# Two more expert lists unsplit: a branch on the lists' lengths and a ring of nine raw buffers

## The chip, the cores and the metric

One NeuronCore of a Trainium2 chip runs the whole program. The metric is device time in microseconds (us) of one execution. TensorE does the matmuls, VectorE (DVE) and ScalarE (ACT) the elementwise work, SyncE's queue (SP) issues the transfers.

## The reference, cut to what matters

A two-layer transformer block over 256 latent tokens and 256 context tokens with 1024 features, all in float32. The second layer ends with a mixture of eight experts on the 256 latent tokens, and the final norm follows it:

```python
logits = h @ router                              # 256 x 8
top_val, top_idx = top_k(logits, 2)
gate = one_hot(top_idx) weighted by softmax(top_val)
out = sum over e of gate[:, e] * ((silu(h @ w1[e]) * (h @ w3[e])) @ w2[e])
```

w1 and w3 are 1024 x 3584 and w2 is 3584 x 1024 for each expert, so all experts together have 352 MB of weights. Each token goes to two experts. With the given inputs the reference's router sends 53 tokens to expert 0; the lists of the other seven have 143, 68, 63, 55, 48, 44 and 38 tokens in order of length.

## The kernel before, in words

The dense part (both mixers, the first layer's FFN, the router) takes the first half of the time; the change leaves it alone. The expert stage follows.

**Slots.** Slot 0 is always expert 0, so that its weights can be fetched before the lists are known. Slots 1 to 7 are the other experts by falling length of list; `rank()` (L921) works out this order on DVE and leaves it in `oi`, and in `ci` by how much each list is too long for its slot. `CAPS` (L35) gives the places of each slot: slots 0, 2 and 3 have one block of 128 rows, slot 1 has blocks of 128 and 64, slots 4 to 7 have 64. Lists that are longer than their slots would be done in a second pass behind a test at the end (L1285), which here is skipped.

**Chunks.** A slot's 3584 hidden features are done in seven chunks of 512. A chunk needs six transfers of 1 MB each (w1 and w3 in two halves each, w2 in two halves), each into one raw buffer of 128 x 2048 floats; there are seven raw buffers.

**Split chunks** (slots 0 to 3). A raw buffer is split into a high part (ACT, L147) and a remainder (DVE, L152), both 2048 wide (`self.wide`), in six w buffers, so in three pairs. For a block of 128 rows `up` (L1087) and `down` (L1125) do three products (high by high, high by low, low by high) and four steps each, so 12 matmuls of 128x512 for a raw buffer; the block of 64 rows carries high and low rows side by side and takes 8. The first matmul of a buffer needs the low part.

**Paired (unsplit) chunks** (slots 4 to 7). `up_pair` (L1057) and `down_pair` (L1078) multiply the raw floats directly, two weight tiles at once in the two halves of the array's columns. The profile shows two records for each such matmul, so 16 records for a call. No conversion is needed; the raw buffer is free when its matmuls are done.

**Order of the work.** `ORDER` (L38) is written out by hand: (slot, number of chunks). Slot 1, which has most matmuls, is strewn between the paired chunks, while slots 0, 2 and 3 run in one piece. Within a step `slots` (L1140) does the hidden activations of the chunk before (`hidden`), the first product, a part of the previous chunk's `down`, and so on; the framework orders each engine's instructions from this. A slot's tokens are gathered by one-hot matmuls (L995) three steps ahead and its outputs are put back into `X` by `combine` or `combine_pair` at its last chunk. `ytile` gives the four PSUM tiles for outputs: a split slot of one block holds two of them over its seven chunks, a paired slot one, and slot 1 takes two for a moment in each `down`.

**The start.** Expert 0 needs no ranking: `places` builds its one-hot matrix, the gather follows, and `rank()`, the second half of `rows` and `gates` are done on DVE beside slot 0's matmuls.

Of the kernel before, what the change touches and what calls it, by code (L numbers as in the profile page):

```python
# [66 lines left out]
NTS = P + 24  # L67
# [8 lines left out]
class Net:  # L76
    def __init__(self, ctx, tc, I, out):
        self.ctx, self.tc, self.nc, self.I, self.out = ctx, tc, tc.nc, I, out
        nc = self.nc
        self.uid = 0  # L80
        self.const = ctx.enter_context(tc.tile_pool(name="const", bufs=1))
        self.cst = self.const.tile([P, NCST], F32, name="cst")
        self.tab = self.const.tile([P, NTA], F32, name="tab")
        self.X = self.const.tile([P, KT, NT], F32, name="X")
        self.mod = [self.const.tile([P, 48, 2], F32, name=f"mod{l}") for l in range(2)]
        self.amp = [[self.const.tile([P, KT, 2], F32, name=f"amp{l}{i}") for i in range(2)] for l in range(2)]
        self.sc = self.const.tile([P, KT, 32], F32, name="sc")
# [9 lines left out]
        self.nw = 0  # L97
        self.ndq = 0
# [32 lines left out]
    def raw(self, src, n=2048):  # L131
        pool, kw = self.stile("raw", F32, 3, 0)
        t = pool.tile([P, 2048], F32, name=self.nm("raw"), **kw)
        self.dq().dma_start(t[:, :n], src)
        return t
# [5 lines left out]
    def split(self, t, n=2048, step=1024):  # L141

        if self.wide:
            hi, lo = self.wtile("whi"), self.wtile("wlo")
            for c in range(0, n, self.wide):
                c = slice(c, c + self.wide)
                self.nc.scalar.activation(hi[:, c], t[:, c], AF.Copy)  # L147
                self.nw += 1

                at = self.urgent if self.nw <= 2 else self.urgent2 if self.nw <= 5 else None  # L150
                with self.tc.issue_after(at) if at else nullcontext():
                    self.nc.vector.tensor_sub(lo[:, c], t[:, c], hi[:, c].bitcast(F32))  # L152
# [768 lines left out]
    def rank(self):  # L921
# [3 lines left out]
        io8, low, over = tab[:, P:P + 8], tab[:, P + 8:P + 16], tab[:, P + 16:P + 24]  # L925
# [24 lines left out]
        self.oi, self.ci = mk("oi", [P, NE], I32), mk("ci", [P, NE + 1], I32)  # L950
        nc.vector.tensor_copy(self.oi, order)
        more = mk("more", [P, NE + 1])
        nc.vector.tensor_sub(more[:, :NE], count, over)
        nc.vector.tensor_scalar(more[:, :NE], more[:, :NE], 0.0, None, ALU.max)
        nc.vector.reduce_sum(more[:, NE:], more[:, :NE], AX.X)
        nc.vector.tensor_copy(self.ci, more)
        for n, v, at in (("sp", pm, self.spos), ("sg", gate, self.sgate)):
            for tt in range(2):
                r = by_slot(f"{n}{tt}", v[:, tt])
                at[tt] += [r[:, q:q + 1] for q in range(1, NE)]  # L960

    def places(self, s, base, width):
# [3 lines left out]
        sp = mo.tile([P, 4], F32, tag="spb" if s == 1 else "sp", name=self.nm("spb"), bufs=2)  # L966
# [8 lines left out]
    def gather(self, s, base, width, first=None, whole=False):  # L975
# [5 lines left out]
        G, sp = first or self.places(s, base, width)  # L981
        GT = mo.tile([P, NL], F32R, tag="GT" + big, name=self.nm("GT"), bufs=2)
# [6 lines left out]
        for part in range(KT // nk):  # L989
            pool, tag = (aux, "x") if part == 0 or not first else (self.hpp, "h")  # L990
# [8 lines left out]
            if whole:  # L999
                self.acopy(xs[0][:, sl], v)  # L1000
            elif width == P:
                ins = self.to_parts(xs[0][:, sl], xs[1][:, sl], v)
                if first and part == 1:
                    self.urgent2 = ins.ins
            else:
                self.to_parts(xs[0][:, sl, :64], xs[0][:, sl, 64:], v)
        if first:
            with self.tc.issue_after(self.urgent):
                self.gates()
# [46 lines left out]

    def up_pair(self, expert, j, kh, x, ps):  # L1057

        mm = self.nc.tensor.matmul
        ws = [self.raw(self.I["moe"][expert, j, 2 * wi + kh]) for wi in range(2)]  # L1060
# [17 lines left out]
    def down_pair(self, expert, j, h, y):  # L1078

        mm = self.nc.tensor.matmul  # L1080
        ws = [self.raw(self.I["moe"][expert, j, 4 + n]) for n in range(2)]
# [5 lines left out]
    def up(self, expert, j, wi, kh, blocks, pss):  # L1087
# [4 lines left out]
        ws = self.weights(self.I["moe"][expert, j, 2 * wi + kh])  # L1092
# [7 lines left out]
    def hidden(self, acts):  # L1100
# [3 lines left out]
        for a in acts:  # L1104
            pt = self.hpp.tile([P, 512], F32, tag="h", name=self.nm("ht"))
            hh = mo.tile([P, 4, P], F32R, tag="hh", name=self.nm("hh"), bufs=3)
# [18 lines left out]
    def down(self, expert, j, n, parts, y, first, last):  # L1125

        mm = self.nc.tensor.matmul
        ws = self.weights(self.I["moe"][expert, j, 4 + n])
# [11 lines left out]
    def slots(self, l, steps, order, caps, base=0, first=None):  # L1140
# [4 lines left out]
        def start(s):  # L1145
            if s and len(self.spos[0]) == 1:
                self.rank()
            if s not in order:
                order[s] = nc.values_load(self.oi[0:1, s:s + 1], engines=[mybir.EngineType.SP], min_val=0, max_val=NE - 1)
            if s not in state:  # L1150
                state[s] = dict(blocks=[self.gather(s, base + b * P, w, None if state else first, paired(caps[s]))
                                        for b, w in enumerate(caps[s])])
# [92 lines left out]

        self.wide = 1024
        for n in range(2):
            finish(todo, n)
        self.wide = 2048

    def experts(self, cx, l, ps):
# [3 lines left out]
        self.extra = (mo, 4, 3)  # L1255
        self.wide = 2048
# [3 lines left out]
        mk("GT", 2, [P, NL], F32R)  # L1260
        mk("sp", 2, [P, 4], F32)
# [4 lines left out]
        mk("rawx", 4, [P, 2048], F32)  # L1266
        self.tabr = mo.tile([P, NTR], F32, name="tabr2")
        mk("wx", 3, [P, 2048], F32R)
# [8 lines left out]
        steps = []  # L1277
        nxt = [0] * NE
        for e, n in ORDER:
            steps += [(e, nxt[e] + i) for i in range(n)]  # L1280
            nxt[e] += n
        self.slots(l, steps, order, CAPS, first=first)
        self.finish()
# [68 lines left out]
def _constants():  # L1352
# [22 lines left out]
    ts[:, P + 16:] = OVER  # L1375
# [112 lines left out]
```

## Time and profile before

| what | us |
|---|---|
| median of three runs (lowest, highest) | 2052.01 (2050.22, 2052.18) |
| the profiled execution's own time | 2054.98 |
| its span, first to last instruction | 2053.2 |
| first gather of the expert stage starts | 980.49 |
| first expert matmul starts | 986.49 |

Times inside an execution count from the first instruction. A busy TensorE is not TensorE at its peak, so a busy share says less than the spacing of equal instructions. The granted clock (PEclk) is given as a share of full speed, 1.00 for 2.4 GHz and 0.50 for 1.2 GHz; a share between is a mean over a stretch with both.

### The profile page before, as it was taken

Reading aid. Unit: us, or ns where it says so; the run is one execution under the profiler, and the core shown is the slowest. Engines: PE = TensorE matmul, PEld = TensorE weight load, DVE = VectorE, ACT = ScalarE, POOL = GpSimd, SP = SyncE. Lnnn points to the kernel's source line nnn. Section 1 sums busy time; section 2 is a strip of 40 time slices with the busy share of each in tenths; the row PEclk is TensorE's granted clock in tenths of the full one; section 3 lists DMA queues with packets and bytes.
Section 4 is the critical chain, followed back from the end, with each engine's and each line's share of the span. In section 5 each row is a group of like instructions: output and inputs, shape, how many; then the busy total and the mean of one; then the engine's idle time right before and its main releaser. Section 6 shows DMA issues by size and latency. Waiting matters only on the chain.

```text
span 2053.2 us, 23609 instructions
## 1 busy us (share of the span) xinstructions
PE 1950.6 (95%) x9254; PEld 1330.5 (65%) x9254; DVE 1030.3 (50%) x1650; ACT 818.6 (40%) x1063; POOL 0.2 (0%) x4
## 2 busy tenths in 40 slices
PE   6999999999999999999899998999999998998996
PEld 4865547778888888557786554554786554784553
DVE  6584455533333367755886222232785224874233
ACT  4574244422222246735674212132674123662121
POOL 0000000000000000000000000000000000000000
PEclk9998999999999999999999999999999999999999
DMA  8310354432322143235898768889997888888783
GB/s 312 129 53 21 113 213 177 185 125 83 131 96 71 62 170 103 87 150 211 312 359 343 297 280 350 344 327 403 355 348 305 327 350 357 336 331 343 289 346 127
DMA packets 68807, 478.43 MB, mean 233 GB/s; under 512 B 7760, under 2 KB 8912, under 8 KB 13392
## 3 DMA queue, kind: packets, MB, share of 16 engines
q1 hardware_dynamic: 68112, 473.03, 59.7%
q10 hardware_dynamic: 576, 3.80, 0.5%
q8 instruction: 75, 1.23, 0.2%
q14 instruction: 44, 0.36, 0.0%
HBM read 475.76 MB, written 1.05 MB: 232 GB/s over the span
## 4 chain that ended last, share of the span: by engine, by line
PE 90%; DVE 4%; ACT 2%; DMA 2%; issue 1%; SPq 0%; ACTq 0%; DVEq 0%
PE ph L1097 18%; PE ph L1063 9%; PE y L1134 9%; PE pf L173 6%; PE pf L175 6%; PE pf L174 6%; PE y L1084 5%; PE pp L175 3%; PE pp L173 3%; PE pp L174 3%; PE ada L200 2%; DVE wlo L152 2%; PE ds L653 2%; PE px L995 1%; ACT whi L147 1%; PE po L173 1%
## 5 line engine op out<-in xcount | busy, mean ns | idle before, releaser
L152 DVE TENSOR_TENSOR wlo<-raw,whi 128x2048 fp32r<-128x2048 f32 x168 | 380.9, 2288 | 198.3 <-ACT whi L147 197.6
L147 ACT ACTIVATE whi<-raw 128x2048 fp32r<-128x2048 f32 x168 | 317.5, 1911 | 59.9 <-PE ph L1097 37.2
L1097 PE MATMUL ph<-whi,xg 128*128 128x512 f32 x1008 | 334.7, 405 | 0.0
L1097 PE MATMUL ph<-wlo,xg 128*128 128x512 f32 x560 | 232.3, 415 | 26.7 <-DVE wlo L152 26.7
L160 DVE TENSOR_TENSOR w<-raw,w 128x1024 fp32r<-128x1024 f32 (+2 forms) x142 | 155.8, 1102 | 179.8 <-ACT w L159 179.6
L159 ACT ACTIVATE w<-raw 128x1024 fp32r<-128x1024 f32 (+2 forms) x142 | 135.5, 961 | 228.8 <-PE pf L175 152.6
L1097 PEld LDWEIGHTS ph<-whi,xg 128*128 128x128 f32 x1008 | 196.4, 195 | 45.6
L1063 PE MATMUL ph<-raw,xn 128*64 128x512 f32 x896 | 223.5, 603 | 2.4 <-DMA raw<-in_moe 2.4
L1097 PEld LDWEIGHTS ph<-wlo,xg 128*128 128x128 f32 x560 | 109.0, 195 | 60.8 <-issue 30.7
L1063 PEld LDWEIGHTS ph<-raw,xn 128*64 128x64 f32 x896 | 64.6, 137 | 115.1 <-issue 108.9
L173 PE MATMUL pf<-fhhi,w 128*128 128x512 f32 x352 | 137.2, 391 | 1.5 <-ACT fhhi L304 1.5
L174 PE MATMUL pf<-fhlo,w 128*128 128x512 f32 x352 | 137.0, 389 | 0.0
L175 PE MATMUL pf<-fhhi,w 128*128 128x512 f32 x352 | 137.0, 389 | 0.0
L1134 PE MATMUL y<-wlo,hh 128*128 128x512 f32 x280 | 113.5, 405 | 6.6 <-DVE wlo L152 6.6
L1084 PE MATMUL y<-raw,hn 128*64 128x512 f32 x448 | 109.9, 596 | 0.9 <-DVE hn L1075 0.9
L1134 PE MATMUL y<-whi,hh 128*128 128x512 f32 x280 | 110.7, 395 | 0.0
L173 PE MATMUL pp<-hhi,w 128*128 128x512 f32 (+1 forms) x272 | 105.0, 386 | 0.0
L101 ACT ACTIVATE act<-ph 128x512 f32<-128x512 f32 x28 | 16.7, 598 | 219.2 <-PE ph L1063 219.2
L175 PE MATMUL pp<-hhi,w 128*128 128x512 f32 (+1 forms) x272 | 104.0, 382 | 0.0
L174 PE MATMUL pp<-hlo,w 128*128 128x512 f32 (+1 forms) x272 | 102.7, 378 | 0.0
L1134 PE MATMUL y<-whi,hl 128*128 128x512 f32 x224 | 89.6, 400 | 0.0
L173 PEld LDWEIGHTS pf<-fhhi,w 128*128 128x128 f32 x352 | 66.0, 188 | 18.4 <-issue 2.5
(329 smaller groups left out, 2813.5 us busy)
## 6 DMA issues: line engine op xcount, KB each, us to landing
raw<-in_moe SPq DMA_DIRECT2D x336, 1024.0 KB, 7.1
raw<-in_ada SPq DMA_DIRECT2D x45, 1024.0 KB, 4.8
raw<-in_ffn SPq DMA_DIRECT2D x22, 1024.0 KB, 4.8
raw<-in_win SPq DMA_DIRECT2D x16, 1024.0 KB, 4.8
raw<-in_ffn SPq DMA_DIRECT2D x16, 704.0 KB, 4.0
raw<-in_wout SPq DMA_DIRECT2D x8, 1024.0 KB, 4.8
raw<-in_winv SPq DMA_DIRECT2D x7, 640.0 KB, 4.8
raw<-in_ada ACTq DMA_DIRECT2D x3, 1024.0 KB, 7.0
```

Source lines behind the costliest of these rows:

```text
L147: self.nc.scalar.activation(hi[:, c], t[:, c], AF.Copy)
L152: self.nc.vector.tensor_sub(lo[:, c], t[:, c], hi[:, c].bitcast(F32))
L159: self.nc.scalar.activation(hi[:, :m], t[:, c:c + m], AF.Copy)
L160: self.nc.vector.tensor_sub(lo[:, :m], t[:, c:c + m], hi[:, :m].bitcast(F32))
L173: mm(out, llo, rhi, start=first, stop=False)
L174: mm(out, lhi, rlo, start=False, stop=False)
L175: mm(out, lhi, rhi, start=False, stop=last)
L200: nc.tensor.matmul(st["ps"][32 * j:32 * j + 32, :], self.sc[:, k, :], w[:, j * 512:(j + 1) * 512], start=k == 0, stop=k == KT - 1)
L1063: mm(ps[64 * wi:64 * wi + 64], x[:, 4 * kh + kk], ws[wi][:, kk * 512:(kk + 1) * 512], start=kh + kk == 0, stop=kh == 1 and kk == 3)
L1084: mm(y[64 * n:64 * n + 64], h[:, f], ws[n][:, f * 512:(f + 1) * 512], start=j == 0 and f == 0, stop=j == NCH - 1 and f == 3)
L1097: mm(ps, xs[x][:, 4 * kh + kk], ws[kk // 2][i][:, kk % 2 * 512:(kk % 2 + 1) * 512], start=kh == 0 and (x, i, kk) == todo[0], stop=kh == 1 ...
L1134: mm(yn, hs[x][:, f], ws[f // 2][i][:, f % 2 * 512:(f % 2 + 1) * 512], start=first and (x, i, f) == todo[0], stop=last and (x, i, f) == to ...
```

## The change

A second table of places, `SHORT`, gives slots 0 and 3 only 64 places, so both become paired, and a second hand-written order, `ORDER_SHORT`, strews the seven chunks of slot 1 and the seven of slot 2 singly between 42 paired chunks. `rank()` also sums by how much the lists are too long for `SHORT` (with 1024 for the slots whose places don't change), now works before the first gather, and ends with the second half of `rows`, `gates` and the positions by slot. All engines load that sum and branch on it: over zero, the old tables, otherwise the new ones. With the lists of the given inputs the sum is zero.

The raw buffers become nine tiles made ahead of the branch and used in turn (six of the expert pool, three of the old stream), and the first nine transfers are issued before the branch. The w buffers go from six to four, and each now holds the high and the low half of 1024 columns (`self.wide` stays 0, so the conversions are 1024 wide, as in the dense part). `hh` goes from 3 to 2, `GT` and `sp` from 2 to 3.

```diff
+SHORT = ((64,), (128, 64), (128,), (64,), (64,), (64,), (64,), (64,))
+ORDER_SHORT = ((0, 3), (1, 1), (0, 3), (2, 1), (0, 1), (3, 2), (1, 1), (3, 3), (2, 1), (3, 2), (4, 1), (1, 1), (4, 3),
+               (2, 1), (4, 3), (1, 1), (5, 3), (2, 1), (5, 3), (1, 1), (5, 1), (6, 2), (2, 1), (6, 3), (1, 1), (6, 2),
+               (7, 1), (2, 1), (7, 3), (1, 1), (7, 1), (2, 1), (7, 2))
...
     def raw(self, src, n=2048):
+        if self.ring:
+            t = self.ring[self.nr[0] % len(self.ring)]
+            self.nr[0] += 1
...
# rank()
+        for c, v in ((NE + 1, short), (NE, over)):
+            nc.vector.tensor_sub(more[:, :NE], count, v)
+            nc.vector.tensor_scalar(more[:, :NE], more[:, :NE], 0.0, None, ALU.max)
+            nc.vector.reduce_sum(more[:, c:c + 1], more[:, :NE], AX.X)
         nc.vector.tensor_copy(self.ci, more)
+        self.rows(1, self.rt["lists"][1][:, :, 0])
+        self.gates()
...
# experts()
-        self.extra = (mo, 4, 3)
-        self.wide = 2048
+        self.extra = (mo, 6, 1)
...
+        self.ring = [mo.tile([P, 2048], F32, name=self.nm("raw")) for _ in range(6)]
+        self.ring += [self.stream.tile([P, 2048], F32, tag="raw", name=self.nm("raw"), bufs=3) for _ in range(3)]
+        self.nr[0] = 0
+        pre = {(i // 6, j): self.raw(self.I["moe"][0, i // 6, j]) for i, j in enumerate((0, 2, 1, 3, 4, 5, 0, 2, 1))}
...
-        first = self.places(0, 0, P)
-        self.urgent = self.rows(1, first[0][:, :, 0]).ins
+        self.rank()
...
+        long = nc.values_load(self.ci[0:1, NE + 1:NE + 2], min_val=0, max_val=2 * NL)
+        with tc.If(long > 0) as c:
+            all_slots(CAPS, ORDER)
+        with c.Else():
+            all_slots(SHORT, ORDER_SHORT)
```

`all_slots` builds the steps from the order, calls `slots` with the tables and then `finish`. The functions `up`, `down`, `up_pair` and `down_pair` take their raw buffer from `part`, which hands out the nine transfers that are already issued and calls `raw` otherwise.

## Rows read from the trace of the kernel before

**Rows 1.** The page's chain that ended last, share of the span by engine.
```profile
PE 90%; DVE 4%; ACT 2%; DMA 2%; issue 1%; SPq 0%; ACTq 0%; DVEq 0%
```
**Rows 2.** Windows: stretch, length, busy PE, PEld, DVE, ACT, POOL, PEclk, DMA share, GB/s.
```profile
986.00:2035.00 1049.00, 992.55 (x4489) 636.37 (x4487) 500.41 (x445) 394.93 (x334) 0.00 (x0) 0.98 0.84 330
...
1050.00:1100.00 50.00, 50.00 (x226) 40.70 (x226) 42.77 (x25) 36.40 (x25) 0.00 (x0) 1.00 0.96 364
...
1400.00:1450.00 50.00, 43.11 (x190) 22.51 (x187) 18.85 (x16) 17.87 (x15) 0.00 (x0) 0.97 1.00 410
```
**Rows 3.** TensorE's waits in the expert stage: us in total, times, longest.
```profile
PE ph L1097 <- DVE wlo L152: 26.7, 8, 3.6
PE ht L1071 <- ACT act L101: 9.5, 13, 0.8
PE y L1134 <- DVE wlo L152: 6.6, 6, 2.5
PE pc L1052 <- DVE X L436: 4.1, 3, 1.4
...
PE ph L1063 <- DMA raw<-in_moe: 2.4, 1, 2.4
```
**Rows 4.** TensorE's timeline, slot 0: the same point of two split chunks in turn.
```profile
1021.13 0.60 PE L1109 MATMUL ht<-tab,act 128*128 128x128 f32 x4
...
1038.26 0.60 PE L1109 MATMUL ht<-tab,act 128*128 128x128 f32 x4
```
**Rows 5.** TensorE's timeline, slot 4: the same point of two paired chunks; idle in brackets.
```profile
1227.77 0.66 PE L1071 MATMUL ht<-tab,act 128*128 128x128 f32 x4 [0.72 <-ACT act L101]
...
1239.66 0.66 PE L1071 MATMUL ht<-tab,act 128*128 128x128 f32 x4 [0.78 <-ACT act L101]
```
**Rows 6.** The timeline, all engines, where a split chunk follows a paired one.
```profile
1420.91 1.90 ACT L147 ACTIVATE whi<-raw 128x2048 fp32r<-128x2048 f32 x1
...
1422.84 2.29 DVE L152 TENSOR_TENSOR wlo<-raw,whi 128x2048 fp32r<-128x2048 f32 x1 [12.14 <-ACT whi L147]
...
1425.28 0.47 PE L1097 MATMUL ph<-wlo,xg 128*128 128x512 f32 x1 [3.56 <-DVE wlo L152]
```
**Rows 7.** Windows, columns as in rows 2: behind two such places.
```profile
1425.00:1430.00 5.00, 4.72 (x14) 3.76 (x15) 4.87 (x4) 1.69 (x1) 0.00 (x0) 0.66 1.00 424
1720.00:1730.00 10.00, 7.42 (x34) 4.89 (x30) 4.92 (x3) 4.58 (x4) 0.00 (x0) 1.00 1.01 428
```
**Rows 8.** TensorE's timeline, the second of these places.
```profile
1727.20 0.50 PE L1097 MATMUL ph<-wlo,xg 128*128 128x512 f32 x1 [1.86 <-DVE wlo L152]
```
**Rows 9.** Groups by form, dense part: conversions 1024 wide; busy, mean ns, idle.
```profile
L160 DVE TENSOR_TENSOR w<-raw,w 128x1024 fp32r<-128x1024 f32 x105 | 127.8, 1221 | 105.3 <-ACT w L159 105.1
L159 ACT ACTIVATE w<-raw 128x1024 fp32r<-128x1024 f32 x106 | 111.3, 1057 | 154.5 <-PE pf L175 98.4 <-PE po L175 18.1 <-DMA raw<-in_win 12.2
```
**Rows 10.** TensorE's timeline: a paired call behind matmuls of a split chunk.
```profile
1207.29 0.40 PE L1134 MATMUL y<-whi,hh 128*128 128x512 f32 x1
1207.62 3.65 PE L1063 MATMUL ph<-raw,xn 128*64 128x512 f32 x16
```
**Rows 11.** DVE's timeline at the start of the expert stage.
```profile
980.77 1.41 DVE L902 SCALAR_TENSOR_TENSOR X<-zt,late,X 128x512 f32<-128x512 f32 x2
...
991.28 0.20 DVE L936 TENSOR_REDUCE rank<-cmp 128x8 f32<-128x64 f32 x1
```
**Rows 12.** TensorE's timeline at the same start.
```profile
980.49 6.24 PE L995 MATMUL px<-G,X 128*128 128x128 f32 x32 [2.02 <-DVE G L972]
986.49 0.48 PE L1097 MATMUL ph<-wlo,xg 128*128 128x512 f32 x1
```
**Rows 13.** The last test, lines L1284 and L1285: ns min/median/max, first and last start.
```profile
L1284 DVEq TENSOR_LOAD <-ci x1: 542/542/542, 2046.8 to 2046.8; - x1
...
L1285 DVEq EVENT_SEMAPHORE  x2: 21/21/21, 2050.8 to 2050.9; - x2
...
L1285 DVEq COMPARE_BRANCH  x1: 72/72/72, 2047.4 to 2047.4; - x1
```

More of the change, by code (lines that the diff above doesn't have):

```diff
@@ L96, in __init__ @@
         self.wide = 0
-        self.nw = 0
+        self.pre = {}
+        self.ring = []
         self.ndq = 0
@@ L973, in places, with gather @@
         return G, sp
-    def gather(self, s, base, width, first=None, whole=False):
+    def gather(self, s, base, width, first=False, whole=False):
         nc, mo, aux = self.nc, self.mo, self.aux
         big = "b" if s == 1 else ""
-        G, sp = first or self.places(s, base, width)
-        GT = mo.tile([P, NL], F32R, tag="GT" + big, name=self.nm("GT"), bufs=2)
+        G, sp = self.places(s, base, width)
+        GT = mo.tile([P, NL], F32R, tag="GT" + big, name=self.nm("GT"), bufs=2 if big else 3)
         if whole:
@@ L989, in gather @@
         for part in range(KT // nk):
-            pool, tag = (aux, "x") if part == 0 or not first else (self.hpp, "h")
+            pool, tag = (self.hpp, "h") if part and first else (aux, "x")
             px = pool.tile([P, 512], F32, tag=tag, name=self.nm("px"))
@@ L1001, in gather @@
             elif width == P:
-                ins = self.to_parts(xs[0][:, sl], xs[1][:, sl], v)
-                if first and part == 1:
-                    self.urgent2 = ins.ins
+                self.to_parts(xs[0][:, sl], xs[1][:, sl], v)
             else:
                 self.to_parts(xs[0][:, sl, :64], xs[0][:, sl, 64:], v)
-        if first:
-            with self.tc.issue_after(self.urgent):
-                self.gates()
         pt = aux.tile([P, 512], F32, tag="x", name=self.nm("gt"))
@@ L1055, in combine_pair, with part @@
                     self.residual(l, 5, 4 * n + 2 * m2 + i, pc[:, i * NL:(i + 1) * NL], NL)
+    def part(self, expert, j, i):
+        if isinstance(expert, int) and (j, i) in self.pre:
+            return self.pre.pop((j, i))
+        return self.raw(self.I["moe"][expert, j, i])
     def up_pair(self, expert, j, kh, x, ps):
         mm = self.nc.tensor.matmul
-        ws = [self.raw(self.I["moe"][expert, j, 2 * wi + kh]) for wi in range(2)]
+        ws = [self.part(expert, j, 2 * wi + kh) for wi in range(2)]
         for kk in range(4):
@@ L1080, in down_pair @@
         mm = self.nc.tensor.matmul
-        ws = [self.raw(self.I["moe"][expert, j, 4 + n]) for n in range(2)]
+        ws = [self.part(expert, j, 4 + n) for n in range(2)]
         for f in range(4):
@@ L1091, in up @@
             pss += [self.hpp.tile([P, 512], F32, tag="h", name=self.nm("ph")) for _ in blocks]
-        ws = self.weights(self.I["moe"][expert, j, 2 * wi + kh])
+        ws = self.split(self.part(expert, j, 2 * wi + kh))
         for ps, (xs, *_) in zip(pss, blocks):
@@ L1127, in down @@
         mm = self.nc.tensor.matmul
-        ws = self.weights(self.I["moe"][expert, j, 4 + n])
+        ws = self.split(self.part(expert, j, 4 + n))
         for b, hs in enumerate(parts):
@@ L1138, in ytile, with slots @@
         return self.yp.tile([P, 512], F32, tag="y", name=self.nm("y"))
-    def slots(self, l, steps, order, caps, base=0, first=None):
+    def slots(self, l, steps, order, caps, base=0, first=False):
         nc, mo = self.nc, self.mo
@@ L1145, in start @@
         def start(s):
[L1146 to L1149, printed above, removed]
             if s not in state:
-                state[s] = dict(blocks=[self.gather(s, base + b * P, w, None if state else first, paired(caps[s]))
+                state[s] = dict(blocks=[self.gather(s, base + b * P, w, first and not state, paired(caps[s]))
                                         for b, w in enumerate(caps[s])])
@@ L1276, in experts, with all_slots @@
         order = {0: 0}
[L1277 to L1283, printed above, removed]
+        for s in range(1, NE):
+            order[s] = nc.values_load(self.oi[0:1, s:s + 1], engines=[mybir.EngineType.SP], min_val=0, max_val=NE - 1)
+        def all_slots(caps, chunks):
+            steps = []
+            nxt = [0] * NE
+            for e, n in chunks:
+                steps += [(e, nxt[e] + i) for i in range(n)]
+                nxt[e] += n
+            assert nxt == [NCH] * NE
+            self.pre = dict(pre)
+            self.slots(l, steps, order, caps, first=True)
+            self.finish()
+        long = nc.values_load(self.ci[0:1, NE + 1:NE + 2], min_val=0, max_val=2 * NL)
[3 more added lines that the diff above has]
+            all_slots(SHORT, ORDER_SHORT)
         more = nc.values_load(self.ci[0:1, NE:NE + 1], min_val=0, max_val=2 * NL)
@@ L1374, in _constants @@
     ts[:, P + 8:P + 16] = [1e7, 700, 600, 500, 400, 300, 200, 100]
-    ts[:, P + 16:] = OVER
+    ts[:, P + 16:P + 24] = OVER
+    ts[:, P + 24:] = [sum(b) if b != a else 1024 for a, b in zip(CAPS, SHORT)]
     tm = np.zeros((P, NTM), f)
```

36 lines of the change are left out of this document (15 added, 21 removed).

## The prediction

> **What bounds the kernel now.** First the chain that ended last: TensorE holds 90% of it [rows 1], so what counts is what TensorE does and what it waits for. Then the windows of the expert stage, 986 to 2035 us: 1049 us long, TensorE busy in 992.6 of them, the transfers at 330 GB/s and a share of 0.84 [rows 2]. So the stage is TensorE's, with the transfers not far behind; in a stretch of 50 us they reached 410 GB/s at a share of 1.00 [rows 2], and 428 in one of 10 us [rows 7]. Last TensorE's waits in the stage [rows 3]: by far the largest is 26.7 us in 8 stops, all for a low part of the weights that DVE has not finished. Only one wait, of 2.4 us, is for a transfer.
>
> Where do the 8 stops come from? The timeline shows one [rows 6]: a split chunk follows a paired one, ACT makes its high part only behind the copy of the paired chunk's activations (1.90 us), DVE then takes 2.29 us for the low part, and TensorE, which starts with that part, idles 3.56 us. Behind it the granted clock of 5 us was 0.66, a mean of both levels [rows 7]: most of it was at 1.2 GHz. At another place the idle was only 1.86 us [rows 8], and the clock stayed at 1.00 [rows 7].
>
> **The branch taken.** The lists sorted as the kernel does it are 53 (expert 0), then 143, 68, 63, 55, 48, 44, 38. Slot 0 has 53 and slot 3 has 63, both at most 64, so the sum that is tested is zero and the new tables run.
>
> **Step A: 14 chunks change from split to paired.** The same point of two split chunks lies 17.13 us apart (1038.26 less 1021.13) [rows 4], of two paired chunks 11.89 (1239.66 less 1227.77), of which 0.78 is the wait for the activation copy [rows 5]: 11.11 of work. 14 x (17.13 - 11.11) = 84.3 us. That wait comes to 9.5 us over the 28 paired chunks of now [rows 3], 0.34 each, since other work often fills it; for 14 more it is 4.8. **Net gain 79.5.** The conversions of these chunks, 84 on each of ACT and DVE, go too; they lay beside matmuls, so that is worth nothing by itself.
>
> **Step B: the stops, 14 where there were 8.** Every split chunk now follows a paired one. But a conversion is 1024 wide: in the dense part ACT takes 1.06 us for it and DVE 1.22 [rows 9], against 1.90 and 2.29, and TensorE can start on the first half. A stop becomes 3.56 - (1.90 - 1.06) - (2.29 - 1.22) = 1.65 us. That lies below the 1.86 us that left the clock alone [rows 8], so I count no clock loss; the seven long stops of now lose 1.7 us each to it (5 us x (1 - 0.66) [rows 7]). Before 26.7 + 11.9 = 38.6, after 14 x 1.65 = 23.1: **gain 15.5.** Bounds: nothing, where the framework puts the conversion ahead of the copy (gain 38.6), to a stop as long as now with its clock loss, 14 x (3.56 + 1.7) = 74 (loss 35). I take 1.65 since rows 8 show such a stop. Four w buffers hold two raw buffers' worth, not three; TensorE needs 2.8 us for one (12 matmuls of 0.233, which is 17.13 less 0.35 for transposes, over 72), the chain of ACT and DVE 2.3, so the depth suffices while a split chunk runs.
>
> **Step C: smaller terms.** Where a paired chunk follows a split one TensorE waited 6.6 us in 6 stops at three such places [rows 3]; there will be seven for slot 2, with shorter conversions: even. Paired slots' last chunks wait for the residual adds, 4.1 us over four slots [rows 3]; two more cost **2**. A change between matmul shapes costs 0.1 us (0.33 us between two starts where 0.233 is usual [rows 10]); seven more strewn chunks with eight such changes: **5.6**. Slot 2 now holds two of the four output tiles while slot 1 wants two for a moment and the paired slot one: one is missing, and a `down` of slot 1 must wait for DVE's add between its blocks, about 1 us, twice in each of six chunks. The paired chunk's matmuls stand ready to fill it; from 0 to 12 us, I take **4**.
>
> **Step D: the start.** Now the gather starts at 980.49 and the first expert matmul at 986.49 [rows 12], and ranking lies beside matmuls. After the change some 37 small DVE operations of 0.13 to 0.20 us (as the reduction of the rank [rows 11]), 4.8 to 7.4 in all, and 1.41 us of row updates [rows 11] stand ahead of the branch: 7.5 us. Then the register load, 0.54, and the branch: at the last test DVE's next instruction came 3.4 us after the branch began (2050.8 less 2047.4) [rows 13]. The other engines pay that at the same time. So the gather starts at 992. It has half the columns, but follows 13 us of idle where the gather of now, 6.24 us [rows 12], followed 2; I take 6.24 again, and 0.75 for the copy: the first matmul at 999.0, **12.5 us later**. Bounds: 9 if the jump costs only the 0.07 us of the instruction, 18 if DVE's operations don't overlap and the clock stays low for the first paired matmuls as well. On SP seven loads of the order and the branch stand before the first transfer of the stage, but nine are issued earlier and the first buffer comes free only after the first paired call, 3.65 us [rows 10]: nothing.
>
> **Step E: the transfers.** All 336 stay: 352 MB in 336 of 1.05 MB, each 2.45 us at 428 GB/s [rows 7]. Three paired chunks take 18 buffers in some 35 us, in which 14.3 arrive; the ring gives the missing 4. Slot 1's chunk (six buffers of 20 matmuls, 28 us, and 2 of transposes) lets 12 arrive for 6; slot 2's (17.9) 7.3 for 6. So three paired, slot 2's, three paired lack 6 to 7 of nine buffers, two of which are in use: just enough. Over eight chunks TensorE needs some 6 x 11.45 + 30 + 17.9 + 3.3 = 120, with gathers and combines 130, the transfers 48 x 2.45 = 118. **I count nothing**; bounds: a gain of 4 if the one wait of now and its clock loss go, a loss of 25 if each of the seven cycles waits 3.5 us.
>
> One rule speaks against this step: the Trainium skill, "DMA: Bandwidth & Descriptors", section "Where 436 GB/s comes from", holds that from HBM about 358 GB/s bind a core. By it a transfer would be 2.93 us and the time, as an estimate, about that of rival 1. Rows 2 and 7 show 410 and 428 from HBM, so the measurement decides.
>
> **Step F: the end.** A second test and the join: one branch more on each engine, mostly beside the last output; 1 us.
>
> **Sum:** 79.5 + 15.5 - 2 - 5.6 - 4 - 12.5 - 1 = 70. The profiled execution took 2054.98 us (span 2053.2, 1.8 outside it); it becomes 1985. That execution is 3 us above the median of 2052.01, so for the median 1982.
>
> **Rivals.**
> 1. *The transfers become the bound.* If no more arrives than beside split chunks, 364 GB/s [rows 2], a transfer takes 2.88 us and the 327 after the first nine 942: from the first freed buffer at some 1002 to 1944. The last paired call, combine, norm and output take some 30 more: 1974. One clock loss of 1.7 us in each of 14 groups of paired chunks adds 24: 1998 in the span, **about 1997** for the median. For: supply and demand are within 10%. Against: that stretch took what TensorE asked for, and rows 7 show more. Chance 0.10.
> 2. *The stops stay long*, since the framework puts both halves on ACT ahead of DVE's first, or other work between: 74 for 23, **2033**. Against: rows 8 show a shorter stop even with the long conversions. Chance 0.10.
> 3. *Paired chunks starve* (slower). Place: each of the 28 paired chunks that follow a paired one. Supply takes 6 x 2.45 = 14.7 us for what TensorE does in 11.5: 3.2 of waiting, nearly the stop of rows 6, and so with the clock loss of 1.7 behind it. 28 x 4.9 = 137: **2119**. It decides from 14 such chunks on (70 / 4.9), so where the ring gives no cover. For: a wait of 2.4 us with seven buffers [rows 3]. Against: it is one in the whole stage, with runs of four paired chunks in it. Chance 0.05.
> 4. *The old tables run*, since the lists on the chip come out otherwise: step A and most of C are gone, eight stops fall from 38.6 to 13.2, and start and end cost 13.5: 2052 - 25 + 13 = **2040**. Against: slot 3's list would have to grow by 2 tokens or slot 0's by 12. Chance 0.04.
>
> The forecast itself has 0.71, with 1955 to 2010 by its bounds (stops, output tiles, start, transfers).
>
> **How the numbers follow.** About 0.2%, 4 us, is what a measurement can tell here. Faster: forecast, rivals 1, 2 and 4 nearly whole, 0.91; same 0.03, the space between rival 2 with more mishaps and no gain; slower 0.06. The range holds the forecast, rival 1 and most of rival 2: 1945 to 2030.
>
> **What would show it.** Right: 42 paired chunks some 11.5 us apart; PE's wait on the low part at 14 stops of 1.5 to 1.9 us with the clock at 1.00; the first expert matmul near 999; no transfer wait over a few us in all; a stage mean near 360 GB/s. Wrong: transfer waits in every cycle (rivals 1, 3), stops of over 3 us (2), 12 matmuls a buffer in slots 0 and 3 (4), or a first matmul past 1005.

## The result, and the profile after

The kernel after takes **1999.12 us** (median of 4 runs, 1997.45 to 2001.74); its ratio to the kernel before is **0.9746, 95% interval 0.9727 to 0.9765**. That is faster by 53 us where 70 was forecast: the forecast of 1982 was 17 us too low, and its range of 1945 to 2030 holds the result. One further run of the kernel before took 3859.22 us and is left out of the ratio. The profiled execution took 2001.74 us, with a span of 2000.0 (before: 2053.2).

First the page of the kernel after: the chain, then three of its groups (busy us, mean ns of one, idle before and its releaser).

```profile
PE 90%; DVE 3%; DMA 2%; ACT 2%; issue 1%; SPq 0%; DVEq 0%; ACTq 0%
...
L1078 PE MATMUL ph<-raw,xn 128*64 128x512 f32 x1344 | 342.0, 609 | 0.0
L1112 PE MATMUL ph<-w,xg 128*128 128x512 f32 x896 | 221.8, 403 | 17.7 <-DVE w L168 17.6
...
L1099 PE MATMUL y<-raw,hn 128*64 128x512 f32 x672 | 164.4, 596 | 0.0
```

TensorE still holds 90% of the chain, as in [rows 1]. The paired matmuls (L1078, L1099) now have 1344 and 672 records, so 126 calls of 16, where 84 ran before: the new tables ran. Now TensorE's waits in the expert stage (us in total, times, longest).

```profile
PE ht L1086 <- ACT act L109: 18.6, 26, 0.7
PE ph L1112 <- DVE w L168: 17.6, 11, 1.6
PE px L1009 <- DVE G L986: 14.1, 1, 14.1
PE y L1149 <- DVE w L168: 9.3, 6, 1.6
PE ht L1124 <- DVE act L1244: 5.5, 7, 0.8
PE pc L1061 <- DVE yl L1052: 5.4, 5, 1.6
PE pc L1061 <- DVE X L444: 4.3, 5, 1.0
```

Against [rows 3] the stops for the low part went from 26.7 us in 8 to 17.6 in 11, those of the down projection from 6.6 to 9.3, and the wait for the copy of a paired chunk's activations doubled from 9.5 to 18.6. The single wait of 14.1 is that for the first gather, in the start. No wait for a transfer is left. The windows say the same (columns as in [rows 2]):

```profile
985.00:1985.00 1000.00, 931.52 (x4192) 498.14 (x4193) 308.13 (x405) 250.06 (x340) 0.00 (x0) 0.97 0.86 345
```

345 GB/s at a share of 0.86, where [rows 2] had 330 at 0.84: the same weights in less time. With no wait for a transfer left, they are not the bound.

**Where the time went.** Each stretch of TensorE's timeline, from the start of one instruction to the start of the next less the idle in brackets, is given to the first of the two. A clock below 1.00 lies inside these times.

| us, profiled executions | before | after | change |
|---|---|---|---|
| up to the first count matmul of the ranking | 977.4 | 975.4 | -2.0 |
| from there to the first expert matmul | 9.1 | 23.9 | +14.8 |
| split matmuls | 574.0 | 334.0 | -240.0 |
| paired matmuls | 318.2 | 479.7 | +161.5 |
| transposes | 41.6 | 44.7 | +3.1 |
| gathers, combines, norm | 62.7 | 66.8 | +4.1 |
| idle of TensorE | 57.3 | 62.2 | +4.9 |
| behind the start of TensorE's last matmul | 13.0 | 13.3 | +0.3 |
| span | 2053.2 | 2000.0 | -53.2 |

The stage from its first expert matmul on gave 66 us, the start took 15 back; 2 us of the 53 lie ahead of the ranking, where nothing was changed. The row that fell short most is the paired one. A call whose matmuls stand in one piece, followed by another such call, takes 3.461 us. Before, the 84 calls took 27.4 us more than that rate; after, the 126 take 43.6 more. This **excess** is 16.2 us larger. The stage fell short by about as much, since 70 and the 12.5 of the start make 82.5 us forecast for it and 66.0 were measured; but the two are not the same thing, as the section on the prediction shows, for a part of the excess is low clock and a part had been forecast. TensorE's timeline of the kernel after shows how one call pays it:

```profile
1361.68 1.07 PE L1078 MATMUL ph<-raw,xn 128*64 128x512 f32 x2
1362.68 2.11 PE L1149 MATMUL y<-w,hh 128*128 128x512 f32 x8
1364.72 3.65 PE L1078 MATMUL ph<-raw,xn 128*64 128x512 f32 x14
1368.30 0.73 PE L1149 MATMUL y<-w,hh 128*128 128x512 f32 x2
```

A call is eight matmuls (two records each), in pairs that use the two halves of the array's columns at the same time. Here the first matmul of a pair runs alone: it takes 1.00 us (1362.68 less 1361.68), eight split ones follow, and the other seven take 3.58 (1368.30 less 1364.72). Together 4.58 us, 1.12 above the rate, since the partner of the first now runs alone too. Such pieces of one matmul stand at 7 places before and 18 after. The rest of the excess are changes between shapes, 153 next to paired groups before and 229 after, and low clock: summed over the clock's records, 1.7 us were lost to it within paired calls before and 6.5 after.

### The profile page after: what moved, and what is told of

Same layout as the page of the kernel before. It is cut to its first block, busy times and chain, and to the rows that moved or that the text cites. A ratio compares the mean times of both kernels' runs of the same rounds, so it can differ in the third digit from the quotient of the medians.

```text
span 2000.0 us, 22801 instructions
## 1 busy us (share of the span) xinstructions
PE 1876.2 (94%) x8918; PEld 1183.0 (59%) x8918; DVE 835.3 (42%) x1633; ACT 664.2 (33%) x1059; POOL 0.2 (0%) x4
## 4 chain that ended last, share of the span: by engine, by line
PE 90%; DVE 3%; DMA 2%; ACT 2%; issue 1%; SPq 0%; DVEq 0%; ACTq 0%
PE ph L1078 16%; PE ph L1112 11%; PE y L1099 8%; PE pf L181 6%; PE pf L182 6%; PE pf L183 6%; PE y L1149 6%; PE pp L183 3%; PE pp L181 3%; PE pp L182 3%; PE ada L208 2%; DMA raw<-in_ada 2%; PE px L1009 2%; PE ds L661 2%; DVE w L168 1%; PE po L181 1%
## 5 line engine op out<-in xcount | busy, mean ns | idle before, releaser
L168 DVE TENSOR_TENSOR w<-raw,w 128x1024 fp32r<-128x1024 f32 (+2 forms) x310 | 354.6, 1166 | 386.8 <-ACT w L167 386.4
L167 ACT ACTIVATE w<-raw 128x1024 fp32r<-128x1024 f32 (+2 forms) x310 | 305.1, 1010 | 259.9 <-PE pf L183 152.6
L1078 PE MATMUL ph<-raw,xn 128*64 128x512 f32 x1344 | 342.0, 609 | 0.0
L1112 PE MATMUL ph<-w,xg 128*128 128x512 f32 x896 | 221.8, 403 | 17.7 <-DVE w L168 17.6
L1112 PEld LDWEIGHTS ph<-w,xg 128*128 128x128 f32 x896 | 167.5, 191 | 72.5 <-issue 26.8
L1078 PEld LDWEIGHTS ph<-raw,xn 128*64 128x64 f32 x1344 | 97.0, 138 | 174.4 <-issue 170.5
L1099 PE MATMUL y<-raw,hn 128*64 128x512 f32 x672 | 164.4, 596 | 0.0
L1149 PE MATMUL y<-w,hh 128*128 128x512 f32 x336 | 106.3, 417 | 9.4 <-DVE w L168 9.3
L1099 PEld LDWEIGHTS y<-raw,hn 128*64 128x64 f32 x672 | 49.0, 137 | 89.9 <-issue 89.3
L1149 PEld LDWEIGHTS y<-w,hh 128*128 128x128 f32 x336 | 62.5, 195 | 47.8 <-DVE w L168 21.0
L181 PEld LDWEIGHTS pf<-fhhi,w 128*128 128x128 f32 x352 | 66.0, 188 | 18.7 <-issue 2.5
L182 PEld LDWEIGHTS pf<-fhlo,w 128*128 128x128 f32 x352 | 66.1, 188 | 13.8 <-DVE fhlo L313 0.3
L183 PEld LDWEIGHTS pf<-fhhi,w 128*128 128x128 f32 x352 | 66.1, 188 | 13.7
L181 PE MATMUL pf<-uhi,w 128*128 128x512 f32 x176 | 68.5, 389 | 0.0
```

The costliest lines, as they stand in the source:

```text
L181: mm(out, llo, rhi, start=first, stop=False)
L182: mm(out, lhi, rlo, start=False, stop=False)
L183: mm(out, lhi, rhi, start=False, stop=last)
L1078: mm(ps[64 * wi:64 * wi + 64], x[:, 4 * kh + kk], ws[wi][:, kk * 512:(kk + 1) * 512], start=kh + kk == 0, stop=kh == 1 and kk == 3)
L1099: mm(y[64 * n:64 * n + 64], h[:, f], ws[n][:, f * 512:(f + 1) * 512], start=j == 0 and f == 0, stop=j == NCH - 1 and f == 3)
L1112: mm(ps, xs[x][:, 4 * kh + kk], ws[kk // 2][i][:, kk % 2 * 512:(kk % 2 + 1) * 512], start=kh == 0 and (x, i, kk) == todo[0], stop=kh == 1 ...
```

## The experiments

Three things have to be known to read them. The part up to the ranking has the same instructions in every kernel, yet took from 967 to 980 us in the profiled executions; so stages are compared from the first expert matmul on. And the clock differs by execution: four runs of one kernel (e10 below) took 1950.4, 1950.6, 1957.0 and 1968.4 us at a mean granted clock of 0.982, 0.982, 0.980 and 0.972. "Clock lost" is the sum, over 5 us windows, of 5 us times what the granted clock lacks to 1.00; the windows begin 11 to 18 us behind the first expert matmul and end 20 to 26 us ahead of the end of the span, so both ends of the stage are left out of it. And e2 to e6 were run once each, so a difference of a few us in their totals says little.

The profiled executions, us:

| | start | stage | stops for the low part | excess of paired calls | clock lost |
|---|---|---|---|---|---|
| before | 9.1 | 1066.7 | 33.3 | 27.4 | 22.2 |
| after | 23.9 | 1000.8 | 26.9 | 43.6 | 13.6 |
| e1 both orders swapped | 24.3 | 951.4 | 2.3 | 24.8 | 10.2 |
| e9 down only | 24.2 | 976.7 | 14.7 | 37.7 | 11.9 |
| e10 up only | 24.2 | 953.4 | 1.1 | 29.0 | 6.8 |
| e11 before, swapped | 9.1 | 1022.8 | 12.7 | 12.9 | 3.4 |
| e7 gather ahead | 20.4 | 1012.2 | 27.0 | 45.4 | 28.9 |
| e8 e7 and e1 | 20.1 | 947.6 | 2.3 | 22.5 | 5.1 |

Start is from the first count matmul to the first expert matmul, stage from there to the end of the span. The last two columns overlap where a paired call ran at the lower clock. Taken up to TensorE's last matmul, both ends included, the clock lost is 22.2 us before and 19.0 after: the kernel after loses 1.9 us more in its first paired calls and 3.4 in its last combine and norm.

**e1, pairs in one piece.** The matmul that needs the later of the two buffers goes first, so that a pair doesn't start before both are there.

```diff
 # up_pair, down_pair
-            for wi in range(2):
+            for wi in (1, 0):
-            for n in range(2):
+            for n in (1, 0):
```

> The changed kernel with the two matmuls of a pair swapped in up_pair and down_pair, so that the one whose weights arrive later comes first; nothing is left out. Theory: in the changed kernel the 126 paired calls take 479.7 us of TensorE's time, 3.81 each, where a call in one piece followed by another takes 3.46; the excess of 43.6 us (27.4 in the kernel before, over 84 calls) is what the forecast left out. 18 of its pieces are about 1 us long, one matmul without its partner. If the order of the pair decides this, no such piece is left and the time falls by 12 to 28 us against the changed kernel, to 1971 to 1988. Rival (the excess is only the change of shape and the clock): under 4 us.

Measured: 1953.32 us (4 runs), ratio to before 0.951 (0.9464 to 0.9557), so 46 us below the kernel after and beyond what was expected. In the compiled order, over both arms of the branch, 67 of 840 pairs were broken in the kernel after and none is here; in the trace no group of paired matmuls is left that is cut inside a pair. The excess fell by 18.8. But the stops fell by 24.6 as well, which no theory had foreseen. Two timelines show why. The kernel after, where a split chunk follows a paired one:

```profile
1259.32 0.60 ACT L109 ACTIVATE act<-ph 128x512 f32<-128x512 f32 x1 [10.10 <-PE ph L1078]
1259.81 1.05 ACT L167 ACTIVATE w<-raw 128x1024 fp32r<-128x1024 f32 x1
...
1260.89 1.23 DVE L168 TENSOR_TENSOR w<-raw,w 128x1024 fp32r<-128x1024 f32 x1 [11.23 <-ACT w L167]
...
1262.27 4.11 PE L1112 MATMUL ph<-w,xg 128*128 128x512 f32 x10 [1.64 <-DVE w L168]
```

The same place of e1:

```profile
1246.62 1.06 ACT L167 ACTIVATE w<-raw 128x1024 fp32r<-128x1024 f32 x1 [3.67 <-DMA raw<-in_moe]
...
1247.71 1.23 DVE L168 TENSOR_TENSOR w<-raw,w 128x1024 fp32r<-128x1024 f32 x1 [4.30 <-ACT w L167]
...
1253.03 0.60 ACT L109 ACTIVATE act<-ph 128x512 f32<-128x512 f32 x1 [5.35 <-PE ph L1078]
...
1254.09 5.17 PE L1112 MATMUL ph<-w,xg 128*128 128x512 f32 x19
```

In the kernel after ACT is idle for 10.10 us behind which stands first the copy of the paired chunk, then the conversion. In e1 the framework put the first conversion ahead of that copy; ACT then waits for nothing but the transfer, DVE's part is done 5 us before TensorE asks for it, and the first split matmul has no idle before it. The swap changed the order on an engine that it doesn't touch. No run moved the conversions alone; e9 and e10 below part the two terms in some measure.

**e2, wide conversions back.**

```diff
 # experts()
         self.extra = (mo, 6, 1)
+        self.wide = 2048
```

> The changed kernel with conversions 2048 wide (two pairs of w buffers); nothing is left out. Theory of step B: the 11 stops of 1.6 us before the first matmul of a split chunk become some 3.5 us and cost 1.7 us of clock behind each, and the 6 stops in down grow as well: 40 to 55 us slower than the changed kernel, 2040 to 2055. Rival (the width of the conversions is hidden by the interleaving): within 5 us of it.

Measured: 2041.92 us, as expected. TensorE's waits in its stage:

```profile
PE ph L1112 <- DVE wlo L160: 38.3, 12, 3.6
```

Twelve stops of 3.2 us where the kernel after has 11 of 1.6; with those of the down projection (2.3 us) 40.6 for 26.9, and 34.2 us of clock lost for 13.6: 13.7 and 20.6 us of the 43 by which its stage is longer. The stops of the down projection fell, from 9.3 to 2.3 us, where they were expected to grow. The half-wide conversions are worth some 43 us once every split chunk follows a paired one.

**e3, seven raw buffers for nine.** Four of the expert pool's in place of six, and seven early transfers.

> The changed kernel with seven raw buffers for nine, seven transfers issued ahead; nothing is left out. Theory: TensorE waits for no transfer in the changed kernel, so nine are more than it needs: 0 to 8 us slower, waits for raw buffers under 8 us in all. Rival 3 of the prediction (paired chunks starve unless the ring covers them): 25 us slower or more, with waits for raw in most cycles.

Measured: 2005.93 us, inside what was expected, but only in total. Waits for transfers come to 1.7 us in the whole stage, none longer than 1.3. Its stage is 14.5 us longer, 10.3 of them clock (23.9 lost), while the part ahead of the ranking happened to be 8 shorter and the start 2.4. The start is shorter because the branch is: with seven early transfers all had landed when TensorE came to it (a DMA share of 0.03 from 975 to 979 us), and it took 3.36 us. The kernel after spends 6.06 there with its transfers still in flight.

```profile
L1301 PEldq COMPARE_BRANCH  x1: 3357/3357/3357, 975.4 to 975.4; - x1
```

Paired chunks don't starve, with nine buffers or with seven.

**e4, the old tables in the new frame.**

```diff
         with c.Else():
-            all_slots(SHORT, ORDER_SHORT)
+            all_slots(CAPS, ORDER)
```

> The changed kernel with the old places and order in both arms of the branch (slots 0 and 3 split, slots 0, 2 and 3 in one piece); nothing is left out. Theory: what is left against the kernel before is the start (15 us later by the trace) and the narrow conversions (25 us by step B's sum, eight stops of 1.65 for 38.6): 2036 to 2046. Rival (the gain comes from ring and conversions, not from the tables): at most 2010.

Measured: 2040.72 us, as expected. Start and branch cost 11 us here (20.1 for 9.1), the stage gave 25.9, and the new tables are worth another 42. So the tables carry most of the gain (42 of 53 us), and not the frame that they stand in.

**e5, no branch.** `all_slots(SHORT, ORDER_SHORT)` stands alone; the test and the arm for longer lists are left out.

> The changed kernel with the new tables alone and no branch on the lists (right only for lists as short as these); nothing else is left out. The first expert matmul starts 23.9 us after the count matmuls in the changed kernel, 9.1 us in the kernel before. Theory: the branch forbids any overlap of ranking and gather, so without it the first matmul follows some 9 to 12 us after the count matmuls and the time is 10 to 15 us less than the changed kernel's, 1985 to 1992. Rival (the table of constants, which lands 16 us after its issue behind nine transfers, is what the start waits for): under 3 us less.

Measured: 1993.41 us, 1.4 above the expected range. And of the 8.5 us by which its span is shorter 5.3 lie ahead of the ranking, where nothing was changed; start and stage together gave 3.2. The start is 23.1 us, only 0.8 less, so the theory missed; the start fits the rival, for without the branch DVE waits for the table of constants:

```profile
983.74 0.48 DVE L986 TENSOR_SCALAR G<-tabr,pm 128x128 f32<-128x128 f32 x2 [5.59 <-DMA tabr<-in_tabr]
```

**e6, the table first.** The transfer of `tabr`, the table for the gather's one-hot matrices, is issued ahead of the nine weight transfers.

```diff
 # experts()
+        self.tabr = mo.tile([P, NTR], F32, name="tabr2")
+        nc.sync.dma_start(self.tabr, self.I["tabr"])
         self.ring = [mo.tile([P, 2048], F32, name=self.nm("raw")) for _ in range(6)]
...
-        self.tabr = mo.tile([P, NTR], F32, name="tabr2")
-        nc.sync.dma_start(self.tabr, self.I["tabr"])
```

> The changed kernel with the transfer of the table tabr issued ahead of the nine raw transfers instead of behind them; nothing is left out. DVE waits 6.7 us for that table at the start, to 989.7, but TensorE's branch instruction lasts until 989.1 as well. Theory (both end at the same time): the first matmul comes at most 2 us earlier, the time within 3 us of the changed kernel's. Rival (the table alone holds the start): 6 us less or more.

Measured: 1999.3 us, as expected, with the same start of 23.9. These two say together what the start waits for. In the kernel after, the branch by its line (ns, start), the table's transfer by its tile, and the timeline:

```profile
L1301 PEldq COMPARE_BRANCH  x1: 6057/6057/6057, 983.1 to 983.1; - x1
```

```profile
DMA to landing us min/median/max: 16.0/16.0/16.0
```

```profile
982.83 0.22 DVE L954 TENSOR_REDUCE sg<-sg_t 128x8 f32<-128x64 f32 x1
...
989.72 0.48 DVE L986 TENSOR_SCALAR G<-tabr,pm 128x128 f32<-128x128 f32 x2 [6.68 <-DMA tabr<-in_tabr]
...
990.16 7.06 PE L1009 MATMUL px<-G,X 128*128 128x64 f32 x32 [14.09 <-DVE G L986]
...
999.25 8.99 PE L1078 MATMUL ph<-raw,xn 128*64 128x512 f32 x32
```

The same three of e6:

```profile
L1301 PEldq COMPARE_BRANCH  x1: 5977/5977/5977, 980.2 to 980.2; - x1
```

```profile
DMA to landing us min/median/max: 2.4/2.4/2.4
```

```profile
986.46 0.48 DVE L986 TENSOR_SCALAR G<-tabr,pm 128x128 f32<-128x128 f32 x2 [6.36 <-issue]
```

The table landed 16.0 us after its issue behind nine transfers of 1 MB, and 2.4 ahead of them. But the branch keeps the engines for 6 us as well, so both let go of DVE at almost the same time; taking either away alone (e5 the branch, e6 the late table) leaves the other.

**e7, the gather ahead of the branch.** The table first, and slot 0's gather of 64 places before the test, with tiles of its own; the ring shrinks to eight for the room.

```diff
 # experts()
+        block = self.gather(0, 0, 64, True, True)
...
         with c.Else():
-            all_slots(SHORT, ORDER_SHORT)
+            all_slots(SHORT, ORDER_SHORT, {0: dict(blocks=[block])})
```

> As the run before, with slot 0's gather for 64 places made ahead of the branch (in tiles of its own; eight raw buffers, for lack of space); nothing is left out. Theory: gather and ranking overlap, TensorE has worked shortly before the branch, and the first expert matmul needs only the branch: 6 to 11 us less than the changed kernel, 1988 to 1994. Rival (branch and code loading hold the start): within 2 us.

Measured: 2004.46 us (4 runs), ratio 0.9771 (0.9737 to 0.9806): 5 us above the kernel after, a miss for the theory and for its rival. The start gained only 3.5 us, since the gather goes first now but the branch still stands ahead of the first expert matmul. And the stage became 11.5 us longer, with the same stops and nearly the same excess: 28.9 us of clock lost where the kernel after loses 13.6. One stop of the kernel after, in TensorE's timeline and in a window over it:

```profile
1433.94 0.73 PE L1149 MATMUL y<-w,hh 128*128 128x512 f32 x2 [1.54 <-DVE w L168]
```

```profile
1432.00:1442.00 10.00, 8.46 (x40) 4.11 (x40) 2.69 (x3) 1.84 (x3) 0.00 (x0) 1.00 0.99 397
```

The same stop in e7:

```profile
1426.80 1.22 PE L1150 MATMUL y<-w,hh 128*128 128x512 f32 x2 [1.55 <-DVE w L169]
```

```profile
1424.00:1434.00 10.00, 7.86 (x30) 4.74 (x32) 2.69 (x3) 2.70 (x4) 0.00 (x0) 0.83 1.00 401
```

The idle is the same to 0.01 us; once the clock stays at 1.00, once it falls and the first two records take 1.22 us for 0.73. All four runs of e7 had a mean clock of 0.971 to 0.974. The kernel after itself shows both: of its 17 stops of 1.50 to 1.64 us before split matmuls five have low clock beside them, as that of 1262.27 above; in e7 it is 11 of the same 17.

```profile
1260.00:1265.00 5.00, 3.36 (x11) 2.61 (x12) 4.11 (x5) 4.01 (x6) 0.00 (x0) 0.75 1.01 419
```

So the stops' length alone doesn't decide; what does is open.

**e8, e7 and e1 together.**

> Gather ahead of the branch, table first, eight raw buffers, and the swapped order within pairs; nothing is left out. If the two gains add: 18 to 39 us less than the changed kernel, 1960 to 1982. If the order within pairs does nothing: as the run before.

Measured: 1942.9 us (4 runs), ratio 0.9483 (0.9447 to 0.9519), better than expected and the fastest of all. That the earlier start of e7 costs nothing here fits the missing stops, behind which e7 lost its clock, but was not tried by itself: 5.1 us of clock lost, and start and stage are 8.1 us below e1's.

**e9 and e10, one swap each**, to part e1's two terms: `down_pair` alone leaves 52 of 840 pairs broken, `up_pair` alone 15, and either moves conversions ahead of copies.

> The kernel after, with the later of the two buffers first in the pairs of the down projection alone. In the compiled order 52 of the 840 pairs stay broken (67 before the edit, none with both swaps), but ScalarE's first conversion of a split chunk now stands ahead of the paired chunk's copy nearly everywhere, as it does with both swaps. Theory (the first swap run gained two separate things: 25 us of stops before split chunks with their clock, by that order of ScalarE, and 19 us of pairs that were broken): this run keeps the broken up pairs and loses the stops, so 20 to 32 us less than the kernel after, 1967 to 1980; 'ph <- w' and 'y <- w' waits of TensorE under 8 us together; time of a paired chunk still about 3.75 to 3.8 us a call. Rival (all of the gain is the broken pairs, the stops went as a consequence): 15 of 67 parts of the 46 us, 1985 to 1992, stops still over 18 us.

> The kernel after, with the later of the two buffers first in the pairs of the up projection alone. 15 of the 840 pairs stay broken and one or two conversions of a split chunk stand ahead of the paired chunk's copy. Theory (stops and broken pairs are two terms): nearly all of the gain of both swaps, 36 to 48 us less than the kernel after, 1951 to 1963; stops under 5 us, 3.66 to 3.72 us a call. Rival (broken pairs alone, 52 of 67 parts of 46): 36 us, 1963, and if the stops stay, over 18 us of waits for 'w'. The two runs together tell the theories apart, not this one alone.

Measured: e9 1975.49 us (0.9635, 0.9596 to 0.9674), e10 1953.8 (0.9542, 0.9493 to 0.9591). Waits of e9:

```profile
PE y L1149 <- DVE w L168: 9.3, 6, 1.6
...
PE ph L1112 <- DVE w L168: 5.4, 6, 1.6
```

and of e10:

```profile
PE y L1149 <- DVE w L168: 1.1, 6, 0.3
```

With only a few pairs mended e9 gains 24 us, so the broken pairs alone can't be the cause: that rival would have given 1985 or more. Its waits are 14.7 us where under 8 was expected, since the `down` ones stayed. From the kernel after to e10 the three columns of the table fall by 25.8, 14.6 and 6.8, together 47.2, and the stage by 47.3; to e9 by 12.2, 5.9 and 1.7, together 19.8 of 24.1. The columns overlap, so that the first sum comes out to 0.1 us is partly luck. But stops and broken pairs don't fall in step: e9 mends 15 of the 67 pairs and loses 12.2 of the 26.9 us of stops, e10 mends 52 and loses 25.8. Stops and broken pairs are two terms, and the clock lost fell in both runs.

**e11, the kernel before with both swaps.** The same edit in the kernel before.

> The kernel before with both swaps: 1 of 336 pairs stays broken (29 before the edit), and the first conversion stands ahead of the paired chunk's copy. Theory (the kernel before paid the same two losses, at its own counts: 33.3 us of waits for 'wlo' and 27.4 us of excess in 84 paired calls): the waits fall to under 8 us, the excess to 14 to 20 us, with some clock, 30 to 50 us less than the kernel before, 2002 to 2022; the branch is then worth 50 to 68 us once the pairs are whole on both sides. Rival (the loss came with the change, by its longer paired runs): within 10 us of the kernel before, 2042 to 2055.

Measured: 2007.46 us (4 runs), ratio 0.9779 (0.9747 to 0.9811): the kernel before paid the same losses. TensorE's waits:

```profile
PE ph L1097 <- DVE wlo L152: 9.0, 7, 1.8
PE y L1134 <- DVE wlo L152: 3.7, 3, 1.2
```

12.7 us remain of 33.3, above the 8 expected, and its excess of 12.9 lies just under the 14 expected; the mean clock was 0.988 to 0.990, the highest of all. In the same set of runs e10, with one of the two swaps, took 1953.8, and e1, with both, 1953.32 in another set: with mended pairs on both sides the branch is worth about 54 us, as much as without.

## Why the prediction was right, and where it was off

**The direction and the frame held.** The stage was TensorE's, transfers were no bound, the new tables ran, and the gain came from step A with the start taken off.

**Step A, mis-sized.** The term was 14 x (17.13 - 11.11). The split side was right: split matmuls fell by 240.0 us, 8.8 of them clock, where 14 chunks at 17.13 less the 0.35 of transposes are 234.9. The paired side failed: 11.11, less 0.59 of transposes, is 10.52 for a chunk or 3.51 for a call, read between the two points of [rows 5], in a run of whole calls. The 42 added calls came to 161.5 us, 3.85 each, and 42 x (3.85 - 3.51) is 14 us. Of these, 4.8 are low clock within paired calls, and 5.6 stood in Step C as changes of shape, so Step A's own share of the 17 us that were missing is 4 to 9. The 84 calls of before had already averaged 3.79, so the profile held the better figure: a mean over all paired calls, not one clean chunk. With slot 2 strewn too, more paired calls stand beside split matmuls that break them. The wait for the copy rose by 9.1, where 4.8 was taken.

**Step B, near in its sum, by luck in part.** The stops are 1.50 to 1.64 us, 1.65 was forecast; 11 before the up projection's first matmul, and still 6 in the down projection, since some places have other work. Stops fell by 6.4 us over both projections and the clock lost, by the table's windows, by 8.6: 15.0 for a forecast of 15.5. But two errors cancel in this. Each of the seven long stops of before was priced at 1.7 us of clock; four cost that and three twice as much, 17.1 together for the 11.9 of the forecast. And the short stops were priced at none; five of 17 cost 1.7 each, 8.5 together. The reason given was wrong: the clock does fall beside some stops of this length, so [rows 8] excluded less than I took from it. Other places took clock that no step counted: three waits for the residual adds (5.1 us, 1.7 before), the first paired calls and the last matmuls. So up to TensorE's last matmul the clock lost fell by 3.2 us where the sum had 11.9. These 8.7 us are about half of the 17 that were missing. The bound "the framework puts the conversion ahead of the copy (gain 38.6)" is what e1 and e10 brought about.

**Step C.** Residual adds: +2.0 us in the two `pc` waits, 2 forecast. The shape changes are real and are part of the excess. The wait of slot 1's `down` for a free output tile, 4 us forecast, doesn't show among the waits. A wait that wasn't forecast does: 5.5 us in 7, for DVE's product in slot 2's chunks.

**Step D, low by 2.3.** 14.8 us for 12.5. Counted from the first count matmul the gather started after 14.8 us, for a forecast of 14.6 (992 less 977.4), but again two errors cancel. DVE's operations overlapped more than I took: the last of the ranking ended at 983.05, 7.7 us behind that matmul, and not 10.6. And I priced the branch by [rows 13] at 3.4 us; it took 6.06 on TensorE with weight transfers in flight. What remains is the gather's 7.06 for 6.24 and 2.0 us from its end to the first matmul where 0.75 was taken. The table's late landing was not in the sum, and cost nothing only because the branch hid it (e6).

**Step E, right.** No wait for a transfer, with nine buffers; 1.7 us with seven. The one wait of 2.4 us of before is gone, with the 1.7 us of clock beside it, which is the gain of 4 that stood as a bound. e1 moved 409 GB/s through 100 us of its stage:

```profile
1500.00:1600.00 100.00, 95.43 (x436) 49.43 (x433) 31.89 (x34) 31.31 (x41) 0.00 (x0) 1.00 0.99 409
```

The some 358 GB/s of the Trainium skill's page "DMA: Bandwidth & Descriptors", section "Where 436 GB/s comes from", is not a bound that this core met.

**Step F, right for the join.** Behind TensorE's last matmul 0.3 us were added, 1 was forecast. What the sum didn't have is that the last combine and norm matmuls ran at a granted clock of 0.50, which cost 3.4 us of the 4.1 by which their row grew:

```profile
1980.00:1985.00 5.00, 5.00 (x14) 3.85 (x13) 1.74 (x5) 3.10 (x6) 0.00 (x0) 0.50 0.00 0
```

A wait of 1.56 us stands a little ahead of them. The kernel before has one of 1.60 at that place and 1.00 behind it, and so have e8 and e9 with the same test and join, so it isn't the branch that does it.

**The rivals.** Rivals 1 and 3 (transfers, starving) fall with e3 and with the waits. Rival 2's mechanism is real, and e2 gives it 2041.92 where 2033 was worked out, but with the narrower conversions the stops stayed short. Rival 4 did not happen; e4 shows it would have been 2040.72, where 2040 was worked out.

## What to carry to other kernels

Price a new instance of an operation by the mean over all present ones, with what breaks and surrounds them, not by the cleanest stretch. Where two matmuls share the array, let the first wait for what arrives last, so that no other work gets between them. After any edit look at the compiled order on the engines it doesn't touch: a conversion behind a copy instead of ahead of it cost more here than the broken pairs (24.6 us of stops for 18.8 of excess, by e1). And price low clock at every stop that the new order keeps, for both short stops and residual waits paid it here at some places.

## What was not expected of the hardware

- A taken branch kept TensorE 6.06 us with nine 1 MB transfers issued ahead and some still in flight (5.98 in e6, 6.22 in e4), and 3.36 to 3.78 us (e3, e8, e7) when all had landed. e3 differs from the kernel after in nothing but the number of buffers and early transfers; by what way they lengthen the branch is not shown.
- A small transfer issued behind nine of 1 MB landed after 16.0 us, ahead of them after 2.4.
- The same 1.55 us stop left the granted clock at 1.00 in one kernel and lowered it in another. All seven stops of 3.5 to 3.6 us of the kernel before had low clock beside them, but of the 17 of 1.50 to 1.64 us five in the kernel after and 11 in e7. The mean clock went from 0.971 to 0.986 between e7 and e8, which differ in the two swaps alone, and 0.010 of it was 18 us within e10's own runs.
- Why the swapped pairs make the framework put conversions ahead of copies, on both kernels, was seen in the compiled order but not explained.
